# Scatter-add of 65,536 edges on one core: the sort's first pass by quads of chunks, its ranks by a ReLU, and a new order of the dense slots

## The chip, the cores and the metric

One core of a Trainium2 chip runs the kernel. The metric is the device time of one execution in microseconds. Before the change it is 392.3 us, the median of 3 runs (391.73 to 395.86).

## What is computed

```python
num_nodes, num_edges, dim = 4096, 65536, 128
for i in range(len(edge_index_src)):
    output[edge_index_dst[i]] += node_features[edge_index_src[i]]
```

Sources and destinations are random node numbers (64-bit in memory, of which the low word is used); features and output are float32, 4096 x 128.

## The kernel before, in words

Nodes are counted in blocks of 128, so an edge has a source block and a destination block (32 of each) and a place within each. The kernel never adds edge by edge. It sorts the edges by destination block, and then makes each block of output by matmuls.

**The features.** X is cut into three bf16 parts, kept negated in the tile x3 and, for the gathers, in a DRAM copy x3d. `x_part(i, v)` (L172) makes part v of quarter i: ScalarE writes the bf16 part (L174); for v = 0 and 1 a GpSimd DMA adds it into the float32 tile xf, which leaves the residual (L176); after part 2, SyncE writes the quarter to x3d.

**Pass 1** sorts by destination block. The 65,536 edges lie as 128 partitions x 512 columns, padded to 528: 24 chunks of 22 columns, six "quads" q of four chunks. For each chunk a one-hot over the 32 destination blocks is built (`oh1s`, 32 VectorE compares for each of two halves of the chunks, L153). An edge's rank is the number of earlier edges in its chunk with the same block: the running count over the columns is made for half 0 by VectorE adds (L357) and for half 1 by TensorE (`counts`, L213), then VectorE multiplies the counts by the one-hot (L236) and TensorE adds over the blocks (L239), which leaves each edge's own rank (`ranks`). `spread1` (L226) multiplies the one-hot by the edge's code and source block. `move1` (L271) then sends each edge to the partition of its rank: VectorE builds a one-hot of the rank, 128 x 2816 for one of the four chunks of a quad (tile p, helper `onehot`, L258), and 22 matmuls per chunk use it as the weights. ScalarE copies the result to sa (codes) and sbk (source blocks).

**Gathers** serve output blocks 0 to 7. `serve(q)` makes the indices from sa and sbk (`gather_keys`), GpSimd issues four indirect DMAs per group (L299; 48 groups in six buffers, which share their pool with xf), VectorE builds a one-hot of the destinations (ohg) and TensorE adds the rows up (`gather_sum`, L313).

**Pass 2 and the dense slots** serve output blocks 8 to 31, in four groups (`GROUPS`). `pass2(g)` is a generator, and each `on(g)` runs it to its next `yield`. In turn: one-hots over the source blocks (oh2, 32 compares, L411); counts by TensorE (psb, L418); v2 and a running sum of 11 adds (L424, L430); a multiply (L434); ranks by TensorE (psr2, L438); then for each pair of output blocks the one-hots p2b (L258), 48 matmuls (ps2, L462), a ScalarE copy (pa, L467) and two small key tiles (L472, L474). A **slot** makes one output block: VectorE builds the tile oh, two one-hots of 128 x 4096 (`onehots`); `blocks` makes 32 count matrices with TensorE (psa, L489), which ScalarE copies to a (L491); `product` multiplies the a of the slot before by X (pso, L495), alternating with `blocks` eight times; VectorE adds the three parts of the block finished before (res, L321 in `finish`) and SyncE writes it out.

The order is written out by hand: each engine works through its own queue in the order in which the code issues instructions, and an instruction waits only for its inputs and for its buffers. PSUM has eight banks: psi 1, psA 3 (psb1, psc, psr, psa), misc 1, psg 1, pso 2. At the end VectorE and TensorE make a flag from the ranks (L552 to L559); every engine loads it and would branch to a general path if a bucket had overflowed.

## Time and profile before

| | |
|---|---|
| median of 3 runs | 392.3 us (391.73 to 395.86) |
| the profiled execution | 397.01 us, its span 395.4 us |
| busy: PE, DVE, ACT, POOL | 315.8, 303.5, 146.1, 226.8 us |
| mean granted TensorE clock | 0.886 |
| instructions in the span | 7887 |

The span runs from the first to the last instruction that the profile shows; the execution's own time is 1.6 us more. PE is TensorE's matmuls and PEld its weight loads, DVE is VectorE, ACT ScalarE, POOL GpSimd and SP SyncE. In the slices each digit is a fortieth of the span. In the groups of instructions, columns are line, engine, operation, tiles and count, then busy us and mean ns of one, then the idle time before them with what ended it. Instructions of one engine overlap a little, so the distance from one start to the next is less than the mean of one.

### The profile page before, as it was taken

What the parts mean: (1) busy time and instruction counts of PE and PEld (TensorE: products, weight loads), DVE (VectorE), ACT (ScalarE), POOL (GpSimd) and SP (SyncE); (2) the same over time, 40 slices, a digit from 0 to 9 for tenths busy, and PEclk for the clock granted to TensorE, in tenths of its full rate; (3) what the DMA queues carried; (4) which work ended last, traced back from release to release, by engine and by line L of the source; (5) the groups of instructions that cost most, each with busy time, mean ns of one, the idle gap of its engine ahead of it and who ended that gap; (6) DMA issues with size and microseconds to landing.
All of it is one profiled execution on the core that took longest, in us unless ns stands there. A gap on an engine that the chain in (4) does not pass through costs nothing.

```text
span 395.4 us, 7887 instructions
## 1 busy us (share of the span) xinstructions
PE 315.8 (80%) x3274; PEld 229.8 (58%) x3274; DVE 303.5 (77%) x532; ACT 146.1 (37%) x271; POOL 226.8 (57%) x216
## 2 busy tenths in 40 slices
PE   0598765797544679676996999999979999999990
PEld 0255664775442567454674777676747776666650
DVE  4998899899899962838799797678898957676310
ACT  2485400100000044132543445455545455546520
POOL 5832038877812777733588777565785775673000
PEclk9999865676675698896998999999999999999995
DMA  8999732232200233321022333232332332332000
GB/s 245 188 162 158 219 120 70 61 81 70 56 17 12 59 82 81 95 57 48 26 57 76 76 86 87 68 80 69 83 78 68 87 92 68 86 87 66 8 14 10
DMA packets 31014, 32.14 MB, mean 81 GB/s; under 512 B 3904, under 2 KB 27648, under 8 KB 30976
## 3 DMA queue, kind: packets, MB, share of 16 engines
q0 software_dynamic: 17536, 23.08, 27.3%
q1 hardware_dynamic: 13296, 8.01, 7.0%
q8 instruction: 26, 0.43, 0.4%
q10 hardware_dynamic: 144, 0.52, 0.4%
q14 instruction: 12, 0.10, 0.1%
HBM read 22.02 MB, written 5.39 MB: 69 GB/s over the span
## 4 chain that ended last, share of the span: by engine, by line
PE 54%; DVE 39%; issue 3%; DMA 1%; ACT 1%; DVEq 0%
PE pso L495 29%; PE psa L489 10%; DVE p L258 9%; PE psg L313 7%; DVE oh L258 6%; DVE v L226 4%; PE ps L462 4%; DVE cum L430 3%; DVE oh L411 3%; DVE oh L153 3%; PE psr L239 2%; DVE cum L357 2%; PE psr L438 2%; DVE v L424 2%; DVE cum L236 2%
## 5 line engine op out<-in xcount | busy, mean ns | idle before, releaser
L299 POOL DMA_INDIRECT rows<-x3d,gidx x192 | 207.3, 1080 | 119.8 <-issue 71.4
L495 PE MATMUL pso<-x,a 128*128 128x384 bf16 x768 | 160.7, 335 | 0.1
L491 ACT CAST a<-psa 128x512 bf16<-128x512 f32 x192 | 111.7, 588 | 109.5 <-PE psa L489 108.6
L489 PE MATMUL psa<-oh 128*128 128x128 bf16 x768 | 76.1, 223 | 13.9 <-DVE oh L258 13.0
L495 PEld LDWEIGHTS <-a 128*128 128x128 bf16 x768 | 69.3, 100 | 28.0 <-issue 3.0
L489 PEld LDWEIGHTS <-oh 128*128 128x128 bf16 x768 | 59.9, 100 | 40.8 <-DVE oh L258 14.4
L258 DVE TENSOR_TENSOR oh<-psi,slo 128x4096 bf16<-128x4096 uint16 x24 | 54.7, 2278 | 0.0
L258 DVE TENSOR_TENSOR oh<-psi,dlo 128x4096 bf16<-128x4096 uint16 x24 | 54.7, 2277 | 0.0
L313 PE MATMUL psg<-rows,ohg 128*128 128x384 bf16 x192 | 41.2, 359 | 14.4 <-DVE ohg L258 13.1
L321 DVE TENSOR_REDUCE res<-pso 128x128 f32<-128x384 f32 x24 | 13.3, 553 | 40.5 <-PE pso L495 40.5
L271 PE MATMUL psm<-v,p 128*128 128x64 bf16 x512 | 34.1, 239 | 10.4 <-DVE p L258 8.8
L258 DVE TENSOR_TENSOR p<-psi,rank 128x2816 bf16<-128x2816 uint16 x24 | 37.5, 1614 | 3.7 <-ACT rank L243 3.7
L271 PEld LDWEIGHTS <-p 128*128 128x128 bf16 x512 | 30.8, 121 | 14.1 <-DVE p L258 13.3
L313 PEld LDWEIGHTS <-ohg 128*128 128x128 bf16 x192 | 19.2, 106 | 28.7 <-DVE ohg L258 14.0
L258 DVE TENSOR_TENSOR p2b<-psi,rank 128x768 bf16<-128x768 uint16 x48 | 23.3, 547 | 14.2 <-PE ps L462 7.4
L176 POOL DMA_DIRECT2D xf<-x x8 | 14.7, 2278 | 13.6 <-ACT x L174 12.2
L462 PEld LDWEIGHTS <-p2b 128*128 128x128 bf16 x576 | 20.0, 102 | 1.8 <-issue 0.3
L258 DVE TENSOR_TENSOR ohg<-psi,gkey 128x512 bf16<-128x512 uint16 x48 | 18.2, 412 | 0.0
L277 ACT CAST sa<-psm 128x128 bf16<-128x128 f32 x6 | 1.6, 266 | 43.4 <-PE psm L271 43.4
L462 PE MATMUL ps<-v,p2b 128*128 128x32 bf16 x480 | 16.9, 197 | 0.0
L174 ACT ACTIVATE x<-xf 128x1024 bf16<-128x1024 f32 x12 | 12.4, 1055 | 7.5 <-DMA xf<-in_node_features_dram 7.5
L411 DVE TENSOR_SCALAR oh<-sbk 128x96 bf16<-128x96 bf16 (+1 forms) x128 | 14.0, 209 | 1.3 <-ACT sbk L278 1.3
(78 smaller groups left out, 234.6 us busy)
## 6 DMA issues: line engine op xcount, KB each, us to landing
xf<-x POOLq DMA_DIRECT2D x8, 512.0 KB, 8.9
x3d<-x SPq DMA_DIRECT2D x4, 768.0 KB, 8.7
rows<-x3d,gidx POOLq DMA_INDIRECT x192, 2.9
xf<-in_node_features_dram SPq DMA_DIRECT2D x4, 512.0 KB, 7.5
out_dram<-res SPq DMA_DIRECT2D x32, 64.0 KB, 1.8
raw<-in_edge_index_src_dram ACTq DMA_DIRECT2D x1, 512.0 KB
raw<-in_edge_index_dst_dram SPq DMA_DIRECT2D x1, 512.0 KB, 5.1
x3d<-zrow SPq DMA_DIRECT2D x1, 96.0 KB, 5.7
```

The source lines that it names most:

```text
L176: G.dma_start(out=xf[i][:], in_=part, accum_op=OP.add)
L226: V.tensor_tensor(out=v1[q][:, :, k], in0=oh1[q // QH][:, :, q % QH], in1=key[:, q, :, None, :].to_broadcast([P, NJ, NB, 4]), op=OP.mult)
L258: V.tensor_tensor(out=dst.rearrange("p i (m k) -> p i m k", k=2), in0=io.rearrange("p i (m k) -> p i m k", k=2), in1=keys2[:, :, None, :]. ...
L271: PE.matmul(out=psm[:, l * 64:(l + 1) * 64], lhsT=p1[:, l % 2, j, :], rhs=v1[q][:, j, :, :, l].rearrange("p k b -> p (k b)"), start=j == j ...
L299: G.indirect_dma_start(out=t[:, l, :], out_offset=None, in_=x3d[:, :], in_offset=bass.IndirectOffsetOnAxis(ap=gidx[:, place(q).start + l, ...
L313: PE.matmul(out=psg[d][:, :3 * P], lhsT=oh[:, l, :], rhs=t[:, l, :], start=q == 0 and l == 0, stop=q == NQ - 1 and l == 3)
L321: V.tensor_reduce(out=res[:], in_=pso[:, :3 * P].rearrange("p (v f) -> p f v", v=3), op=OP.add, axis=AX.X, negate=True)
L411: V.tensor_single_scalar(out=oh2[:, :, :, s, :], in_=sbk[:, :, ds].rearrange("p c (i k) -> p c i k", k=4), scalar=float(s + 1), op=OP.is_e ...
L462: PE.matmul(out=ps2[:, d % per * NB:(d % per + 1) * NB], lhsT=p2b[d % 2][:, c, :], rhs=v2[:, c, d // 4, :, d % 4], start=c == 0, stop=c == ...
L489: PE.matmul(out=psa[:, i * P:(i + 1) * P], lhsT=oh[0][:, s, :], rhs=oh[1][:, s, :], start=True, stop=True)
L491: S.copy(out=a[:, k * 4:k * 4 + 4, :], in_=psa[:].rearrange("p (s m) -> p s m", s=4))
L495: PE.matmul(out=pso[:, :3 * P], lhsT=a[:, s, :], rhs=x3[:, s, :, :].rearrange("p v f -> p (v f)"), start=s == 0, stop=s == NB - 1)
```

## The change

Pass 1 is done quad by quad. For each quad VectorE builds one one-hot with the helper `onehot` (one instruction of 128 x 2816, which reads the PSUM copy of iota) in place of the compares. TensorE sums each column over the partitions (`pst`, 22 matmuls of one column), VectorE takes a running sum of the 22 totals (`scan`), and TensorE forms the counts in PSUM from the matrix `early`, which is the strict triangle with 4096 on the diagonal, plus the totals of the columns before. ScalarE evicts them with ReLU and a bias of -4096, so that only an edge's own block keeps a count, its rank; the running adds and the multiply of VectorE are gone. The adds over the blocks, the spread, and the move remain, with other layouts: blocks are innermost now, so the move's right-hand side is contiguous.

The residuals of X are made by 16 GpSimd `tensor_tensor` adds of 128 x 512 in place of eight accumulating DMAs. In the slots, VectorE builds the tile oh for slot i+1 before TensorE's slot i, the table `STEPS` says which step of which pass-2 group runs in which slot, GROUPS becomes (4, 4, 8, 8), keys are made pair by pair, and the gather sums come last in a slot while their one-hots are built earlier (`prepare`). The flag is made one slot before the last. PSUM: psA 2, psg 2.

```diff
-GROUPS = (4, 8, 8, 4)
+GROUPS = (4, 4, 8, 8)
+STEPS = {0: [(1, 2)], 1: [(1, 2)], 2: [(1, 0)], 3: [(1, 0), (2, 1)], 4: [(2, 2)], 5: [(2, 1)],
+         6: [(2, 0)], 7: [(2, 0)], 9: [(2, 0), (3, 1)], 11: [(2, 0)], 12: [(3, 2)], 13: [(3, 1)],
+         14: [(3, 0)], 16: [(3, 0)], 18: [(3, 0)], 20: [(3, 0)]}
...
         if v < 2:
-            G.dma_start(out=xf[i][:], in_=part, accum_op=OP.add)
+            for h in range(2):
+                bs = slice(h * BX // 2, (h + 1) * BX // 2)
+                G.tensor_tensor(out=xf[i][:, bs], in0=xf[i][:, bs], in1=part[:, bs], op=OP.add)
...
+    def oh1s(q):
...
+        onehot(oh1q(q), kd[q][:], NL, NB)
+        pst = ps.tile([P, 512], F32, name="pst", tag="pso")
+        for j in range(NJ):
+            PE.matmul(out=pst[:, j:j + 1],
+                      lhsT=oh1q(q)[:, 4 * j:4 * j + 4, :].rearrange("p l b -> p (l b)"),
+                      rhs=ones[:, :1], start=True, stop=True)
...
+    def scan(q):
...
+        V.tensor_tensor_scan(out=sums[q][:], data0=ones[:, :NJ], data1=pst[:, :NJ], initial=0.0,
+                             op0=OP.mult, op1=OP.add)
...
+    def counts(q):
...
+        for j0 in range(0, NJ, 4):
+            n = min(4, NJ - j0)
+            psc = ps.tile([P, 512], F32, name="psc", tag="psA")
+            PE.matmul(out=psc[:, :n * P], lhsT=early[:],
+                      rhs=oh1q(q)[:, 4 * j0:4 * (j0 + n), :].rearrange("p t b -> p (t b)"),
+                      start=True, stop=j0 + n == 1)
+            for j in range(max(j0, 1), j0 + n):
+                PE.matmul(out=psc[:, (j - j0) * P:(j - j0 + 1) * P],
+                          lhsT=sums[q][:, j - 1:j].to_broadcast([P, P]), rhs=identb[:],
+                          start=False, stop=j == j0 + n - 1)
+            S.activation(out=cum[:, :, 4 * j0:4 * (j0 + n)], func=RELU, bias=minus[:],
+                         in_=psc[:, :n * P].rearrange("p (t b) -> p b t", b=NB))
+            yield
...
+        for b in range(NB):
+            PE.matmul(out=psr[:, :NL], lhsT=identb[:], rhs=cum[:, b, :],
+                      start=b == 0, stop=b == NB - 1)
...
+    for q in range(3):
+        dst_keys(q)
+    x_part(0, 0)
+    oh1s(0)
+    codes()
+    x_part(1, 0)
+    oh1s(1)
+    scan(0)
...
+    def during(q):
+        def step(l):
+            if q + 2 < NQ:
+                count(q + 2, 2 if l < 3 else 99)
+            if q == 0:
+                x_part(*((2, 1), (3, 1), (0, 2), (1, 2))[l])
+            elif q == 1 and l < 2:
+                x_part(2 + l, 2)
+        return step
+    for q in range(NQ):
+        move1(q, during(q))
+        if q + 3 < NQ:
+            oh1s(q + 3)
+        if q + 1 < NQ:
+            spread1(q + 1)
...
+        if q + 3 < NQ:
+            scan(q + 3)
+        if q >= 3:
+            add_up(2 * q - 5)
...
+    for slot, (g, i) in enumerate(flat_slots):
+        steps = STEPS.get(slot, ())
+        n = n0 + (len(order) - n0) * (slot + 1) // slots
+        for pg in pending:
+            on(pg)
+        pending = [pg for pg, k in steps if k == 0]
+        prepare(n)
+        cur = oh
+        if slot + 1 < slots:
+            oh = onehots(*flat_slots[slot + 1])
+        for pg, k in steps:
+            for _ in range(max(k - 1, 0)):
+                on(pg)
+                on(pg)
+            on(pg)
+        finish()
...
+        for k in range(8):
+            blocks(k, cur, a)
+            if prev is not None:
+                product(k, prev[1], prev[2])
...
+        for pg, k in steps:
+            on(pg)
+        add_up(n)
+        prev = (first[g] + i, a, pso)
+        if slot == slots - 2:
+            flag()
```

How it moves the queues is shown at three places, each before and then changed. The first is VectorE from the one-hot of the last edges to the first one-hots of the move (p); cum, v, oh and sums are pass 1's tiles, and the numbers behind names are buffers.

```order
L153 TENSOR_SCALAR oh_131<-kd_124 128x66x4 x32
L226 TENSOR_TENSOR v_243<-oh_130,ka 128x22x128
L226 TENSOR_TENSOR v_243<-oh_130,kb 128x22x128
L357 TENSOR_TENSOR cum_210<-cum_210,oh_130 128x384 x4
L226 TENSOR_TENSOR v_250<-oh_130,ka 128x22x128
L357 TENSOR_TENSOR cum_210<-cum_210,oh_130 128x384 x8
L226 TENSOR_TENSOR v_250<-oh_130,kb 128x22x128
L357 TENSOR_TENSOR cum_210<-cum_210,oh_130 128x384 x9
L236 TENSOR_TENSOR cum_210<-cum_210,oh_130 128x4224 x2
L258 TENSOR_TENSOR p_486<-psi,rank_236 128x2816 x2
```

```order
L196 TENSOR_TENSOR oh_292<-psi,kd_129 128x2816
L257 TENSOR_TENSOR v_317<-oh_147,ka 128x88x32
L257 TENSOR_TENSOR v_317<-oh_147,kb 128x88x32
L220 SCALAR_TENSOR_TENSOR sums<-ones,pst 128x22
L196 TENSOR_TENSOR p_408<-psi,rank_284 128x2816
L196 TENSOR_TENSOR p_408<-psi,rank_284 128x2816
L196 TENSOR_TENSOR p_489<-psi,rank_284 128x2816 x2
L196 TENSOR_TENSOR oh_292<-psi,kd_130 128x2816
L257 TENSOR_TENSOR v_614<-oh_147,ka 128x88x32
L257 TENSOR_TENSOR v_614<-oh_147,kb 128x88x32
L220 SCALAR_TENSOR_TENSOR sums<-ones,pst 128x22
L196 TENSOR_TENSOR p_620<-psi,rank_399 128x2816
```

The 21 running adds and the multiplies are gone, the next quads' one-hots stand between the moves, and ahead of each quad's first p stands a scan (L220), which reads TensorE's pst of a later quad.

The second is ScalarE in the same stretch; x is a part of X, cum the evicted counts, rank the copied ranks.

```order
L174 ACTIVATE x_199<-xf 128x8x128 x4
L185 ACTIVATE kb<-raw 128x528
L186 ACTIVATE ka<-raw 128x528
L200 CAST cum_210<-psb_212 128x384
L215 CAST cum_211<-psc 128x384 x4
L174 ACTIVATE x_199<-xf 128x8x128
```

```order
L236 ACTIVATE cum<-psc,minus 128x32x16 x5
L236 ACTIVATE cum<-psc,minus 128x32x8
L245 CAST rank_284<-psr 128x88 x2
L178 ACTIVATE x_135<-xf 128x8x128 x2
L236 ACTIVATE cum<-psc,minus 128x32x16 x2
L178 ACTIVATE x_135<-xf 128x8x128
L236 ACTIVATE cum<-psc,minus 128x32x16 x3
L236 ACTIVATE cum<-psc,minus 128x32x8
L245 CAST rank_399<-psr 128x88 x2
L178 ACTIVATE x_135<-xf 128x8x128
```

The parts of X, all four first parts of which stood ahead of everything, now stand in between the evictions of the counts, and half 0's counts go through ScalarE too.

The third is VectorE around the first dense slot; oh is the slot's pair of one-hots, oh_1278 and oh_1774 (32 compares) the start of pass 2 for the second group.

```order
L411 TENSOR_SCALAR oh_1218<-sbk 128x24x4 x32
L411 TENSOR_SCALAR oh_1278<-sbk 128x48x4 x32
L288 TENSOR_SCALAR gslo<-sa 128x32
L289 TENSOR_SCALAR gkey<-sa 128x64
L291 SCALAR_TENSOR_TENSOR gidx<-sbk,gslo 128x32
L424 TENSOR_TENSOR vc_1217<-oh_1218,sa 128x3072
```

```order
L196 TENSOR_TENSOR oh<-psi,slo_1624 128x4096
L196 TENSOR_TENSOR oh<-psi,dlo_1625 128x4096
L504 TENSOR_SCALAR slo_1624<-pa 128x128
L506 TENSOR_SCALAR dlo_1625<-pa 128x128
L196 TENSOR_TENSOR ohg<-psi,gkey 128x512
L196 TENSOR_TENSOR oh<-psi,slo_1624 128x4096
L196 TENSOR_TENSOR oh<-psi,dlo_1625 128x4096
L442 TENSOR_SCALAR oh_1774<-sbk 128x24x4 x32
L456 TENSOR_TENSOR v_1775<-oh_1774,sa 128x3072
```

The second group's start has moved from right behind the first group's to behind the one-hots of the first two slots, and it has four output blocks in place of eight.

More of the change, by code (lines that the diff above doesn't have):

```diff
@@ L247, in place @@
[L247 to L253 removed]
+    oh1, sums, rank1, v1 = {}, {}, {}, {}
     def onehot(dst, keys2, n, m=P, io=None):
```

365 lines of the change are left out of this document (161 added, 204 removed).

## The prediction

> **What bounds the kernel now.** I read the page's engine totals and slices first, then the chain of waits in order of time, then the groups of pass 1, and last the timeline of single engines.
>
> ```profile
> span 395.4 us, 7887 instructions
> PE 315.8 (80%) x3274; PEld 229.8 (58%) x3274; DVE 303.5 (77%) x532; ACT 146.1 (37%) x271; POOL 226.8 (57%) x216
> PE   0598765797544679676996999999979999999990
> DVE  4998899899899962838799797678898957676310
> PEclk9999865676675698896998999999999999999995
> ```
>
> No engine bounds the whole. VectorE is full in the first 14 slices (to 140 us) while TensorE is half busy and its clock is low; from slice 21 (210 us) on TensorE is full. The chain of waits gives the landmarks:
>
> ```profile
> 0.93 5.08 DMA raw<-in_edge_index_dst_dram
> 41.01 3.21 DVE p L258 x3
> 100.79 7.01 DVE oh L411 x64
> 148.50 1.13 PE pso L495 x4
> 181.86 1.28 PE pso L495 x4
> 256.16 0.65 PE pso L495 x4
> 257.03 0.65 PE pso L495 x4
> 379.88 5.21 PE pso L495 x32
> ```
>
> The edges are there at 6.0, the first p of the move starts at 41.0. Pass 1 ends at 100.8, where pass 2 starts its compares. The first product (slot 1) is at 148.5, that of slot 10 at 256.2, and the last product runs from 379.9 to 385.1. So the span falls into 100.8 for pass 1, 47.7 of preparation, 107.7 for slots 1 to 9, 123.7 for slots 10 to 23, and 15.5 of tail. An eighth of a slot takes 0.87 at full clock (256.16 to 257.03), a slot 7.0. Nine slots in 107.7 is far from that: TensorE waits for VectorE there, and pays again when it restarts at a low clock:
>
> ```profile
> 213.72 0.61 PE L489 MATMUL psa<-oh 128*128 128x128 bf16 x4 [3.13 <-DVE oh L258]
> 180.00:182.50 2.50, 1.25 (x7) 0.86 (x8) 2.50 (x5) 0.55 (x1) 1.89 (x3) 0.50 0.35 81
> ```
>
> The first is a TensorE wait of 3.13 us for a slot's one-hots. The second is the window behind such a wait (columns PE, PEld, DVE, ACT and POOL busy, then the granted clock, 0.50): there the four products took 1.28 instead of 0.65. Two or three eighths at that pace cost about 1.7 us.
>
> **Pass 1.** These rows carry it:
>
> ```profile
> L258 DVE TENSOR_TENSOR p<-psi,rank 128x2816 bf16<-128x2816 uint16 x24 | 37.5, 1614 | 3.7 <-ACT rank L243 3.7
> L226 DVE TENSOR_TENSOR v<-oh,ka 128x2816 bf16<-128x2816 bf16 x6 | 9.7, 1616 | 0.0
> L153 DVE TENSOR_SCALAR oh<-kd 128x264 bf16<-128x264 bf16 x64 | 10.9, 298 | 0.0
> L357 DVE TENSOR_TENSOR cum<-cum,oh 128x384 bf16<-128x384 bf16 x21 | 7.5, 357 | 0.6
> L236 DVE TENSOR_TENSOR cum<-cum,oh 128x4224 bf16<-128x4224 bf16 x4 | 9.2, 2349 | 0.0
> L174 ACT ACTIVATE x<-xf 128x1024 bf16<-128x1024 f32 x12 | 12.4, 1055 | 7.5 <-DMA xf<-in_node_features_dram 7.5
> L243 ACT CAST rank<-psr 128x132 bf16<-128x132 f32 x8 | 2.1, 350 | 13.9 <-PE psr L239 13.9
> 141.18 4.04 ACT L491 CAST a<-psa 128x512 bf16<-128x512 f32 x8
> L142 DVE TENSOR_SCALAR raw<-raw 128x528 int32<-128x528 int32 x1 | 0.4, 436 | 3.1 <-DMA raw<-in_edge_index_dst_dram 3.1
> 98.87 1.43 PE psm L271 x21
> 300.70 1.37 PE psr L438 x32
> ```
>
> Removed from VectorE: 10.9 + 7.5 + 9.2 = 27.6 us. Added: six one-hots of 128 x 2816, each like p, whose 24 take 37.5 or 1.55 each: 9.3. Six key shifts of 176 columns are bounded by nothing and by the 0.44 of 528 columns; I take 0.25, 1.5 together. Six scans of 22 columns cost at least 0.1 and at most one 0.44; I take 0.2, 1.2 together. VectorE is thus 15.6 lighter, and a quad costs it seven instructions of 1.55, 10.9.
>
> But the work on the counts moves to ScalarE: 33 evictions of 512 columns (six per quad, the last half as long, so 5.5). A plain one takes 0.50 (4.04 for eight). The ReLU reads PSUM with a stride, as the rank copies do, which need 350 for 132 columns. I bound it by 0.50 and by that rate, 350 / 132 x 512 = 1.36, and take 0.65: a fixed part is most of the 350, and the plain row is the nearer in size. In order, then:
>
> - VectorE from 6.0: three shifts 0.75, a one-hot 1.55, three code operations about 2, a one-hot 1.55, scan, three shifts, scan, one-hot 1.55, spread 3.1: at 18 it waits. TensorE meanwhile sums 44 columns and forms quad 0's counts (5.5 x 1024 columns; at full clock 0.43 for 1024, by row psb further down, 24 x 256 columns in 2.65; at half clock 4.7 in all), ScalarE follows, the 32 rank matmuls take about 1.4 (row psr, 96 columns) to 2.4, then come the next 22 sums that scan(2) reads. The first p starts at about 21.5. It was 41.0, but with the one-hots of all edges done.
> - VectorE then has p(0), one-hot, spread, 10.9, to 32.4. The next scan reads sums that stand behind quad 0's last move in TensorE's queue, and this behind the counts of quads 1 and 2, which ScalarE evicts in between the parts of X. From 20.5 ScalarE has eight of them (8.4 with the row's 1.055), two quads of evictions (7.2), rank copies (1.2), and about 2 of waits for rank matmuls: it ends at 39.5. So VectorE stands for 7.
> - From 39.5: quad 1 10.9 and two sets of gather keys 1.5; from quad 2 on a p has 2688 columns and a quad's four take 5.9, so quad 2 11.3 with keys, quads 3 and 4 9.7 and 10.1 without a one-hot but with gather one-hots, quad 5 5.9; 2.0 from the last p to the compares, as before (98.8 to 100.8). TensorE's share of a quad is 88 moves at 0.068 (row psm) = 6.0, counts 2.4, ranks 1.4 and sums 1.5, 11.3 in all, beside VectorE's, without adding. The sum is 91.
>
> Pass 1 gives **-9.8**. Bounds: with 0.50 for the ReLU, and TensorE and ScalarE nowhere in the way, the 7 us vanish (84); with 1.36, 16.5 evictions up to the scan add 11.7, and nothing is gained.
>
> **The adds on GpSimd.** Sixteen adds of 128 x 512 are in no row. The nearest:
>
> ```profile
> masks.py:199 POOL TENSOR_SCALAR_AFFINE_SELECT ident<-ident 128x128 f32<-128x128 f32 x1 | 0.3, 285 | 0.0
> L163 DVE TENSOR_SCALAR raw<-raw 128x528 int32<-128x528 int32 x1 | 1.0, 1040 | 0.0
> L299 POOL DMA_INDIRECT rows<-x3d,gidx x192 | 207.3, 1080 | 119.8 <-issue 71.4 <-PE psg L313 42.6 <-PE psa L489 4.3
> ```
>
> 285 for 128 columns of one input gives 1.14 for 512; two inputs make at most 2.28; a quarter of the 1.14 is the other end. I take 1.14. ScalarE reads each residual, so the last part of X may wait: after 22.6, when the last first part is written, twelve adds remain, and ScalarE wants the last result at 43.5. That fits while an add costs up to 1.75, and costs nothing; at 2.28 it is 6.5 late. By the Trainium skill (GPSIMD Engine Reference, 3.1 Elementwise) a float32 add of 2048 columns took 4497 ns, so an estimate is 1.1 us here, and by it too the sum stays.
>
> L163 is the same shift as L142 on as many columns and took 1040 instead of 436, while GpSimd was writing descriptors: the two engines get in each other's way. The Trainium skill (SBUF — State Buffer, Who interferes with whom) says that a VectorE instruction with two SBUF inputs and a GpSimd one that reads SBUF exclude each other for their whole length; that is a rule against these adds. It hits only the spreads: the one-hots read iota from PSUM. By that rule the four spreads of 1.6 between 15 and 32 us delay the adds by 6.5 at most, the last one then ends at 22.6 + 13.7 + 6.5 = 42.8, and the sum is the same.
>
> The gathers start when x3d is written, behind ScalarE's last part of X:
>
> ```profile
> 40.81 3.88 ACT L174 ACTIVATE x<-xf 128x1024 bf16<-128x1024 f32 x4
> ```
>
> This part ends at 44.6 after the change, against 44.7, so they move little; 192 of them in 207.3 busy, 119.8 idle, are not the bound.
>
> **Preparation.** Pass 2's first group has the same VectorE work as before, but the second group's stands behind the one-hots of slots 0 and 1. These rows price it and the slots:
>
> ```profile
> 191.26 3.89 DVE L411 TENSOR_SCALAR oh<-sbk 128x192 bf16<-128x192 bf16 x32
> 203.92 5.01 DVE L430 TENSOR_TENSOR cum<-cum,oh 128x512 bf16<-128x512 bf16 x11
> L434 DVE TENSOR_TENSOR cum<-cum,oh 128x6144 bf16<-128x6144 bf16 x2 | 6.7, 3345 | 0.0
> L258 DVE TENSOR_TENSOR oh<-psi,slo 128x4096 bf16<-128x4096 uint16 x24 | 54.7, 2278 | 0.0
> 128.60 1.50 PE ps L462 x48
> 222.36 2.65 PE psr L438 x32
> 198.87 2.78 PE L418 MATMUL psb<-oh,before 128*128 128x256 bf16 x24
> 281.72 1.31 PE psg L313 x8
> ```
>
> For four blocks: compares 3.1 (7.01 for both sets, less 3.89), v2 and multiply 1.7 each (half of 3.3), running sum 3.5, p2b 1.9 per pair. In order from pass 1's end: 3.1 compares, 0.4, 1.7 v2, 1.4 wait for counts, 3.5, 1.7, 3.4 for psr at half clock and its copy, 3.9 for three gather sums at half clock, 1.5 ps, 1.7 copy, keys and gather one-hots, 1.9 p2b, 4.4 oh for slot 0, 0.6, 4.4 oh for slot 1, 3.1 compares of the second group. Only then does TensorE reach its psb, which its queue has ahead of slot 0: 2.6, then slot 0 at ScalarE's pace 4.5, a gather sum and psa 1.1. The sum is 44.9, **-2.8**. If the compares stood behind slot 0 it would be 5.7 less; if TensorE is at half clock still in slot 1, 1.7 more.
>
> **Slots 1 to 9.** TensorE's own work: nine slots 62.8; 14 gather groups at 0.65, 9.1; five ps at 1.5, 7.6; psr 1.4 and 2.65, two psb of 2.65: 88.9. Its waits for VectorE, which may be one slot ahead but not more (oh has two buffers): for the second group's multiply at the end of slot 1, 1.6; for the third group's compares at the end of slot 3, 2.5; for its multiply at the end of slot 5, 4.2, since v2 3.4, running sum 5.0 and multiply 3.3 come on top of three oh of 4.4. Of the two longer ones I let one drop the clock, 1.7. That is 98.9, **-8.8**. Bounds: no wait at all, 88.9, and all as before, 107.7.
>
> **Slots 10 to 23.** 97.7 + 14.6 for gather groups + 2.65 + five ps 7.6 + a wait of 3.9 for the fourth group's multiply (as in slot 5) = 126.5, **+2.8**: the eight-block group now comes last, and its pairs fall here. Bounds +/-4.
>
> **Tail.**
>
> ```profile
> 385.11 0.56 DVE L321 TENSOR_REDUCE res<-pso 128x128 f32<-128x384 f32 x1 [4.64 <-PE pso L495]
> 386.62 0.14 DVE L559 TENSOR_SCALAR flag_i<-fone 1x1 int32<-1x1 f32 x1
> ```
>
> The flag's chain from 385.7 to 386.8 goes under the last slot: **-1.1**, or 0 if the output's DMA is what the end waits for.
>
> **Sum.** -9.8 - 2.8 - 8.8 + 2.8 - 1.1 = -19.7, a span of 375.7. The profiled execution took 1.6 more than its span and, at 397.0, 4.7 more than the median, so I apply the difference to the median: 392.3 - 19.7 = **372.6 us**.
>
> **Rivals.**
> - *ScalarE is not in the way.* Its waits overlap better than I let them, and VectorE leads without a stop: -7 in pass 1, and half of the 10 of waits and clock in slots 1 to 9: 360.6. For it speaks that ScalarE is busy 37%; against it the queue order, eight parts of X amid the evictions. Chance 0.17.
> - *Counts hold pass 1.* ReLU at 1.36, or TensorE at half clock (counts, ranks, sums and moves doubled are more than VectorE's 10.9): the 9.8 are gone, 382.4. For it speaks PEclk of 5 to 7 tenths in those slices; against it that TensorE would be full then. 0.13.
> - *VectorE gets no slot ahead*, because it waits for ps copies and buffers: slots 1 to 9 stay at 107.7, 381.4. For: it must wait for pa after slots 2 and 6. Against: the next oh is built already. 0.08.
> - *GpSimd's adds hold ScalarE* (slower). Place: ScalarE's last parts of X, with quad 3's evictions behind them. Beyond 1.75 us every add costs twelvefold; at 3.4 the gain is gone; at 4, 372.6 + 27 = 399.6. Against: it is over twice the nearest row. 0.07, of which 0.05 beyond 1%.
> - My forecast, 364 to 380: 0.55.
>
> Within 1% (388.4 to 396.2) is about what a measurement can tell from no change. Faster 0.91, same 0.04, slower 0.05. The range goes from 358 (most of what the first rival may give, 372.6 - 7 - 10 = 355.6) to 386 (the second with three clock drops).
>
> **What would show it.** Right: one-hots of 1.55 in pass 1, the first p near 21, a VectorE stop of several us ahead of quad 1's p, compares near 91, first product near 136, slot 10 near 235, last product near 361. Wrong: a ReLU above 1 us; a GpSimd add above 2; a TensorE wait for oh in slots 1 to 9; the first p after 30.

## The result, and the profile after

| | before | predicted | after |
|---|---|---|---|
| median of all runs, us | 394.08 (4 runs) | 372.6 (358 to 386) | 368.78 (4 runs, 368.19 to 369.46) |
| ratio to before | 1 | | 0.938, 95% interval 0.931 to 0.945 |
| pass 1, to the compares of pass 2 | 100.8 | 91.0 | 87.5 |
| preparation, to slot 1's first product | 47.7 | 44.9 | 42.9 |
| slots 1 to 9 | 107.7 | 98.9 | 98.0 |
| slots 10 to 23 | 123.7 | 126.5 | 129.5 |
| tail, from the start of the last 32 products | 15.5 | 14.4 | 8.6 |
| span of the profiled execution | 395.4 | 375.7 | 366.4 |

The change is 6% faster, within the range. In a later session it took 367.64 us beside 396.3 for the kernel before. In some sessions every kernel, the one before included, took about a fifth longer (before: 481 to 484) from some 55 us of the span on; of the runs there I read what lies before 55 us and single places named below. Where a run is set against the changed kernel of another session (367.6 to 368.8, before 394 to 396), the difference is good to about 2 us.

The page of the changed kernel, totals and three slice rows (slices of 9.2 us):

```profile
span 366.4 us, 8352 instructions
PE 299.4 (82%) x3527; PEld 219.8 (60%) x3527; DVE 287.0 (78%) x476; ACT 160.2 (44%) x297; POOL 224.5 (61%) x225
PE   0768867656373597979989999997799999999996
DVE  4982899999759689699994799659994959687721
PEclk9978988978565699989999999999899999999999
```

VectorE lost 16.5 us of busy time (303.5 before), near the 15.6 worked out for pass 1. TensorE's fell by as much (315.8 before), most of it in the moves, below. TensorE is at 7 to 9 tenths from the slice at 128 us on; before, it was full only from 210 on. The chain of waits, in order of time, gives the landmarks of the table:

```profile
87.45 3.16 DVE oh L442 x32
228.39 0.65 PE pso L530 x4
357.85 5.21 PE pso L530 x32
363.08 0.56 DVE res L333
```

What VectorE does and waits for up to quad 2 (five rows of its timeline; in brackets the idle time before a row and what ended it), and GpSimd beside it:

```profile
13.54 1.91 DVE L257 TENSOR_TENSOR v<-oh,ka 128x2816 bf16<-128x2816 bf16 x1
15.37 2.57 DVE L257 TENSOR_TENSOR v<-oh,kb 128x2816 bf16<-128x2816 bf16 x1
19.41 6.19 DVE L196 TENSOR_TENSOR p<-psi,rank 128x2816 bf16<-128x2816 uint16 x4
37.60 0.20 DVE L220 TENSOR_TENSOR_SCAN sums<-ones,pst 128x22 bf16<-128x22 bf16 x1 [7.40 <-PE pst L211]
49.30 5.92 DVE L196 TENSOR_TENSOR p<-psi,rank 128x2688 bf16<-128x2688 uint16 x4
```

```profile
12.81 3.66 POOL L182 TENSOR_TENSOR xf<-xf,x 128x512 f32<-128x512 f32 x2 [1.24 <-ACT x L178]
```

The first p starts at 19.4 (predicted 21.5, before 41.0). The stop of 7.40 us ahead of quad 1's p is there, where and as long as predicted (7). Behind it VectorE's timeline has no wait over 0.25 us up to the last move: from quad 1 on it is full, with quad 2's p at 49.3. TensorE's waits of over 1.3 us from 120 us to the end (its timeline) are these five:

```profile
122.69 2.74 PE L449 MATMUL psb<-oh,before 128*128 128x128 bf16 x24 [9.39 <-DVE oh L442]
139.25 1.53 PE L474 MATMUL psr<-cum,identb 128*128 128x96 bf16 x32 [2.18 <-DVE cum L470]
162.15 4.46 PE L449 MATMUL psb<-oh,before 128*128 128x256 bf16 x24 [2.45 <-DVE oh L442]
184.65 2.82 PE L474 MATMUL psr<-cum,identb 128*128 128x192 bf16 x32 [1.40 <-DVE cum L470]
259.07 1.44 PE L530 MATMUL pso<-x,a 128*128 128x384 bf16 x4 [4.98 <-DVE res L333]
```

All five come from counting work of a later group, as the prediction had them in slots 0, 1, 3, 5 and 13; none is a slot's own one-hots. In the fifth a product needs a buffer that res frees, and on VectorE res stands behind that group's values v2 and running sum (250.2 to 258.5 us), not behind its multiply. The third and the fifth are paid twice. The view by stretches shows the clock right behind them (the column ahead of the DMA share and GB/s):

```profile
162.15:166.61 4.46, 4.46 (x26) 3.32 (x27) 4.46 (x6) 0.00 (x0) 0.00 (x0) 0.62 0.06 18
259.07:262.00 2.93, 2.93 (x13) 1.59 (x13) 2.93 (x4) 0.59 (x1) 2.32 (x3) 0.52 0.45 113
```

At a mean clock of 0.62 the 24 sums took 4.46 instead of the 2.78 of before, and at 0.52 the first four products 1.44 instead of 0.65. The operations that were new, by groups (instructions | busy, mean ns of one | idle before):

```profile
L236 ACT ACTIVATE cum<-psc,minus 128x512 bf16<-128x512 f32 (+1 forms) x36 | 22.0, 656 | 12.2 <-PE psc L233 11.8
L182 POOL TENSOR_TENSOR xf<-xf,x 128x512 f32<-128x512 f32 x16 | 19.8, 1275 | 11.3 <-ACT x L178 11.3
L280 PE MATMUL psm<-v,p 128*128 128x64 bf16 x512 | 20.6, 200 | 4.9 <-DVE p L196 4.8
```

The ReLU took 0.66 (taken: 0.65), the add 1.28 (1.14). The moves of quads took 20.6 for 512, 0.040 each, not the 0.068 that I had taken from before.

### The profile page after: what moved, and what is told of

Its sections match the earlier page's. It is cut to its first block, busy times and chain, and to the rows that moved or that the text cites. A ratio compares the mean times of both kernels' runs of the same rounds, so it can differ in the third digit from the quotient of the medians.

```text
span 366.4 us, 8352 instructions
## 1 busy us (share of the span) xinstructions
PE 299.4 (82%) x3527; PEld 219.8 (60%) x3527; DVE 287.0 (78%) x476; ACT 160.2 (44%) x297; POOL 224.5 (61%) x225
## 4 chain that ended last, share of the span: by engine, by line
PE 55%; DVE 36%; ACT 5%; DMA 1%; issue 1%; DVEq 0%
PE pso L530 27%; DVE oh L196 10%; PE psa L524 9%; DVE p L196 8%; PE psg L325 6%; PE ps L496 4%; DVE cum L465 3%; DVE v L257 3%; DVE oh L442 3%; PE psr L474 3%; PE psb L449 2%; ACT cum L236 2%; DVE v L456 2%; PE psr L241 1%; ACT x L178 1%; DVE cum L470 1%
## 5 line engine op out<-in xcount | busy, mean ns | idle before, releaser
L306 POOL DMA_INDIRECT rows<-x3d,gidx x192 | 199.8, 1041 | 101.2 <-issue 48.1
L530 PE MATMUL pso<-x,a 128*128 128x384 bf16 x768 | 156.3, 328 | 5.5 <-DVE res L333 5.5
L196 DVE TENSOR_TENSOR p<-psi,rank 128x2688 bf16<-128x2688 uint16 (+1 forms) x24 | 36.1, 1566 | 0.0
L236 ACT ACTIVATE cum<-psc,minus 128x512 bf16<-128x512 f32 (+1 forms) x36 | 22.0, 656 | 12.2 <-PE psc L233 11.8
L182 POOL TENSOR_TENSOR xf<-xf,x 128x512 f32<-128x512 f32 x16 | 19.8, 1275 | 11.3 <-ACT x L178 11.3
L280 PE MATMUL psm<-v,p 128*128 128x64 bf16 x512 | 20.6, 200 | 4.9 <-DVE p L196 4.8
L449 PE MATMUL psb<-oh,before 128*128 128x128 bf16 (+1 forms) x96 | 12.3, 309 | 14.7 <-DVE oh L442 11.8
L280 PEld LDWEIGHTS <-p 128*128 128x128 bf16 x512 | 18.6, 103 | 6.9 <-DVE p L196 6.5
L496 PEld LDWEIGHTS <-p2b 128*128 128x128 bf16 x576 | 19.7, 101 | 3.6 <-DVE p2b L196 2.1
L233 PEld LDWEIGHTS <-sums 128*128 128x128 bf16 x126 | 12.1, 116 | 14.4 <-issue 6.6
L449 PEld LDWEIGHTS <-before 128*128 128x128 bf16 x96 | 10.0, 127 | 17.2 <-DVE oh L442 12.7
```

The costliest lines, as they stand in the source:

```text
L182: G.tensor_tensor(out=xf[i][:, bs], in0=xf[i][:, bs], in1=part[:, bs], op=OP.add)
L196: V.tensor_tensor(out=dst.rearrange("p i (m k) -> p i m k", k=2), in0=io.rearrange("p i (m k) -> p i m k", k=2), in1=keys2[:, :, None, :]. ...
L236: S.activation(out=cum[:, :, 4 * j0:4 * (j0 + n)], func=RELU, bias=minus[:], in_=psc[:, :n * P].rearrange("p (t b) -> p b t", b=NB))
L280: PE.matmul(out=psm[:, l * 64:(l + 1) * 64], lhsT=p1[:, l % 2, j, :], rhs=v1[q][:, 4 * j + l].rearrange("p k b -> p (k b)"), start=j == 0, ...
L306: G.indirect_dma_start(out=t[:, l, :], out_offset=None, in_=x3d[:, :], in_offset=bass.IndirectOffsetOnAxis(ap=gidx[:, place(q).start + l, ...
L449: PE.matmul(out=psb[:, h * W:(h + 1) * W], lhsT=before[:], rhs=flat2(oh2)[:, h * NH + c], start=c == 0, stop=c == NH - 1)
```

## Experiments

Two theories were open. Theory A: the prediction's terms, each at its size, the tail for 1.1. Theory B: the tail is the miss, since what the program does with the flag after it is written was most of the empty end. Beside them each term of pass 1 and the lead of a slot has its own rival.

**1. The flag early in the kernel before** (`e1_before_flag_early`). The chain becomes a function and is called in the loop:

```
             prev = (first[g] + i, a, pso)
+            if slot == slots - 1:
+                flag()
         on(g + 1, 99)
```

> The kernel before with one edit: the flag's chain stands after the gather blocks of slot 23, ahead of the last 32 products, as it does after the change; nothing else is altered. Theory A, the prediction's term: only the chain of small instructions from 385.7 to 386.8 goes under the products, so the time falls by about 1.1 us. Theory B: what the program does with the flag after it is written (the engines load it to branch on it) is most of the 8.6 us that the profile shows empty from 386.8 to 395.4, and runs beside the last products once the flag is early, so the time falls by 6 to 7 us and the span ends about 3 us after the last reduction of res.

Measured: 393.0 us, ratio 0.997 (0.993 to 1.002): no difference. The call stood one slot earlier than meant, behind slot 22's blocks (slot was counted up above it). VectorE and TensorE there, and the end of the chain of waits:

```profile
372.04 0.28 DVE L510 TENSOR_REDUCE fone<-psf 1x1 f32<-1x128 f32 x1 [7.56 <-PE psf L508]
376.95 0.61 PE L489 MATMUL psa<-oh 128*128 128x128 bf16 x4 [4.94 <-DVE oh L258]
```

```profile
387.33 5.21 PE pso L495 x32
392.57 0.56 DVE res L321
```

VectorE waits 7.56 us for the transposed maximum, which stands behind slot 22's blocks in TensorE's queue. Slot 23's one-hots stand behind that wait, so TensorE then waits 4.94 for them. The last 32 products start at 387.3 instead of 379.9, 7.4 later, but the end is 395.9: the tail is 8.6 instead of 15.5. The 7 us were gained at the end and lost in slot 23. That the total stands still is no evidence for theory A.

**2. The same, past the one-hots** (`e9_before_flag_early2`), in one of the slower sessions:

```
             oh = onehots(g, i)
             finish()
+            if slot == slots - 1:
+                flag()
```

> The kernel before with the flag's chain moved again, now right behind the one-hots of slot 23 on VectorE and ahead of slot 23's blocks on TensorE, so that no one-hots stand behind its wait for the transposed maximum (in the first try the chain stood after slot 22's blocks, VectorE waited 7.6 us for that transpose and slot 23's one-hots came 5 us late). Theory B (loading the flag after it is written is what the 8.6 us of empty end were): slot 23 starts as it did before plus about 1 us, the end follows the last reduction by about 3 us, and the time falls by 5 to 7 us against the kernel before. Theory A (chain alone): by about 1 us.

Measured: ratio 0.979 (0.959 to 1.000), 469.1 against 480.9; the interval reaches 1, so the total alone decides nothing, and the tail does. Slot 23 is no longer held up (VectorE waits 0.58 for the transpose, TensorE for no one-hots), and the page's first line and the end of the chain read:

```profile
span 466.0 us, 7887 instructions
```

```profile
457.37 5.21 PE pso L495 x32
462.61 0.56 DVE res L321
```

The tail is 8.6 here too, and the span ends 2.8 us after the last reduction. In place and size this is theory B: with the flag written early, all but 2.8 us of the empty end is gone.

**3. The flag late in the changed kernel** (`e2_after_flag_late`):

```
-        if slot == slots - 2:
-            flag()
     finish()
     for k in range(8):
         product(k, prev[1], prev[2])
     done.append((prev[0], prev[2]))
     finish()
+    flag()
```

> The changed kernel with the flag's chain put back behind the last slot's reduction and output. Theory A (chain alone): plus 1.1 us, about 370. Theory B (the load of the flag costs the end): plus 6 to 7 us, about 375, with 8 to 9 us of empty span behind the flag's last instruction.

Measured: 379.22 us, 10.4 over the changed kernel (368.78, another session). The page's first line and two rows of the chain:

```profile
span 378.4 us, 8353 instructions
```

```profile
364.13 0.56 DVE res L333
366.68 0.14 DVE flag_i L545
```

The spans differ by 12.0: 1.0 lies ahead of the last products, 2.1 is the chain (364.7 to 366.8), and 8.8 is an empty stretch of 11.6 us behind the flag in place of the 2.8 behind the last reduction. So theory B has the sign and the place, and its 6 to 7 are too little here: in the changed kernel the early flag is worth about 10 us.

What stands in the empty stretch is in the kept traces, among the instructions that the views leave out (start in us of the span, then duration):

| | before | flag late (run 3) | changed |
|---|---|---|---|
| flag written, end | 386.76 | 366.82 | 350.05 |
| GpSimd loads the flag | 386.79, 0.50 | 366.86, 0.50 | 350.09, 0.50 |
| GpSimd `INC_SWDGE_SEM` | 388.27, 1.38 | 368.31, 1.91 | 351.55, 1.91 |
| GpSimd `DRAIN` | 389.68, 4.89 | 370.25, 7.10 | 353.49, 7.10 |
| span ends | 395.4 | 378.4 | 366.4 |

Each of the five engines loads the flag in about half a microsecond and branches. GpSimd, behind its branch, then ends its part of the program with these two instructions, 6.3 us in the kernel before and 9.0 in the changed one, and the engines meet behind them, 0.8 to 1.0 us ahead of the end. So it is not the loads that fill the stretch: GpSimd's end waits for the flag, and with the flag early it runs beside the last products. In all fourteen kept traces the two instructions take 1.38 and 4.89 us where X's residuals are made by DMAs (before, and runs 1, 2, 8 and 9) and 1.91 and 7.10 where GpSimd adds them. Those 2.7 us, brought by the adds, are nearly all of the 2.9 by which the stretch of run 3 is longer than that of the kernel before. Why the adds lengthen GpSimd's end, nothing here shows.

**4. No slot ahead** (`e3_after_own_slot`):

```
-    oh = onehots(0, 0)
...
-        cur = oh
-        if slot + 1 < slots:
-            oh = onehots(*flat_slots[slot + 1])
+        cur = onehots(g, i)
```

> The changed kernel with VectorE's lead of one slot taken away: a slot's one-hots are built in the slot itself, behind whatever VectorE did in the slot before. Theory (the lead is what slots 1 to 9 gained): TensorE waits for oh at several of the early slots, 2 to 4 us each with low-clock products behind, and slots 1 to 9 go from 98.0 back to about 107; preparation loses nothing, since slot 1's one-hots no longer stand ahead of the second group's compares (4.4 earlier); slots 10 to 23 change by less than 3. In all plus 5 to 9 us, about 376. Rival: the lead does nothing, TensorE's waits for the groups' multiplies are the whole cost of these slots: 366 to 370, with slots 1 to 9 at 98.

Measured: 429.28 us, 60 over the changed kernel and 8.5% over the one before (ratio 1.086, 1.077 to 1.095). Preparation takes 38.3 us, 4.6 less, as expected; slots 1 to 9 take 123.5 instead of 98.0, slots 10 to 23 170.1 instead of 129.5. Rows of the view of waits from slot 1 on (us in total, times, longest), without and then with the slot ahead:

```profile
DVE slo L504 <- ACT pa L500: 78.1, 10, 9.5
PE psa L524 <- DVE oh L196: 56.8, 13, 6.0
```

```profile
DVE slo L504 <- ACT pa L500: 29.8, 8, 4.9
```

In this order of steps pass 2's products ps, which place the edges of a pair of output blocks, stand behind a slot's blocks on TensorE, so VectorE waits for their copy pa until the slot ends. With the next one-hots already built this wait is free. Without them the 4.4 us of one-hots come behind the wait, and TensorE stands 13 times for 56.8 us. Theory and rival both had this far too small: the kernel before builds a slot's one-hots in the slot itself too, and by the same view its TensorE waited for them 5 times, 13.0 us in all, and VectorE twice for pa, 7.8. Its steps stand elsewhere. The new order needs the lead; without it, it is worse than the old one.

**5. X's parts later** (`e4_after_x_late`), and with them the first two sets of gathers:

```
-    count(1, 2)
-    x_part(0, 1)
     count(1)
-    x_part(1, 1)
     scan(2)
...
         def step(l):
             if q + 2 < NQ:
                 count(q + 2, 2 if l < 3 else 99)
-            if q == 0:
-                x_part(*((2, 1), (3, 1), (0, 2), (1, 2))[l])
-            elif q == 1 and l < 2:
-                x_part(2 + l, 2)
+            if q in (1, 2):
+                x_part(l, q)
...
-        if q == 1:
+        if q == 2:
             serve(0)
-        if 1 <= q < NQ - 1:
+            serve(1)
+        if 2 <= q < NQ - 1:
             serve(q)
```

> The changed kernel with the parts of X moved in ScalarE's order: the second parts during quad 1's move, the third during quad 2's, so that six of them no longer stand ahead of quad 1's ranks; the gathers of the first two gather groups are issued two quads later. Theory of the prediction (ScalarE's queue, evictions amid parts of X, makes VectorE stand 7.4 us ahead of quad 1's p): six parts at 1.06 leave this queue, the stop falls to 1 to 3 us and quad 1's p starts near 33 instead of 37.6; some of that may be lost later, as the first gather comes at about 60 instead of 49. Rival 1 (TensorE at low clock sets quad 1's counts and sums): the stop stays at 6 to 7 us. Rival 2 (VectorE bounds the rest anyway and the late gathers hold nothing): the end moves by all that the stop loses, to 362 to 364 us. If the later evictions of X collide with quads 3 and 4, the gain is given back and the time is 368.

Measured: 373.6 us, 4.8 over the changed kernel.

```profile
33.77 0.20 DVE L220 TENSOR_TENSOR_SCAN sums<-ones,pst 128x22 bf16<-128x22 bf16 x1 [3.92 <-PE pst L211]
63.02 1.11 POOL L306 DMA_INDIRECT rows<-x3d,gidx  x1 [14.40 <-issue]
110.47 0.23 DVE L500 TENSOR_SCALAR slo<-pa 128x128 uint16<-128x128 uint16 x1 [4.81 <-ACT pa L496]
```

The stop goes from 7.40 to 3.92 us, less of a fall than expected (1 to 3 left), and quad 1's p starts 3.8 earlier, at 33.9: six of the eight parts of X make about half of the stop. The first gather is issued at 63.0 instead of 49.2, and GpSimd, at one gather in 1.25 us, does not catch up by the preparation: the chain of waits runs over its gathers from 85 to 105 us, VectorE waits 4.81 for pa (2.95 in the changed kernel), and preparation takes 47.4 instead of 42.9. The early parts of X cost 3.8 at quad 1 and buy more than that. The edit moves the gathers with the parts, so the two are not told apart.

**6. One spread more per quad** (`e5_extra_spread`; the same values written twice), in a slower session:

```
-        for k, key in ((0, kab), (1, kb[:])):
+        for k, key in ((0, kab), (1, kb[:]), (1, kb[:])):
```

> The changed kernel with the second product of each of pass 1's six spreads done a second time into the same place (same result): about 1.55 us more VectorE per quad, nothing else. Prediction's theory (VectorE stands idle ahead of quads 0 and 1, and from quad 2 on it is what sets each p): the extra ones ahead of the stops vanish, the four for quads 2 to 5 add 1.55 each, the compares start 6 us later (93.5), and this reaches the end: about 375. Rival 1 (ScalarE or TensorE sets the later quads too): compares at 87.5 to 89. Rival 2 (VectorE sets everything from the start): plus 9.3, compares at 96.8.

```profile
37.53 0.20 DVE L220 TENSOR_TENSOR_SCAN sums<-ones,pst 128x22 bf16<-128x22 bf16 x1 [4.67 <-PE pst L211]
50.90 5.92 DVE L196 TENSOR_TENSOR p<-psi,rank 128x2688 bf16<-128x2688 uint16 x4
```

The extra spread ahead of quad 0 uses up the wait of 1.35 there (p at 19.57 instead of 19.41), and the one ahead of quad 1 vanishes in its stop (4.67 left of 7.40, p at 37.65). Quad 2's p comes at 50.90 instead of 49.30, later by the one spread behind quad 1's p. So VectorE sets quad 2 and does not set quads 0 and 1, as predicted. For quads 3 to 5, the compares and the end (479.75) this run can't be read; that VectorE sets them rests on its full timeline, above.

**7. Each ReLU eviction twice** (`e6_relu_twice`; same values), in a slower session:

```
-            S.activation(out=cum[:, :, 4 * j0:4 * (j0 + n)], func=RELU, bias=minus[:],
-                         in_=psc[:, :n * P].rearrange("p (t b) -> p b t", b=NB))
+            for _ in range(2):
+                S.activation(out=cum[:, :, 4 * j0:4 * (j0 + n)], func=RELU, bias=minus[:],
+                             in_=psc[:, :n * P].rearrange("p (t b) -> p b t", b=NB))
```

> The changed kernel with each ReLU eviction of pass 1 done twice into the same place (same result): 33 more ScalarE instructions of 0.66, 22 us in all, four or so us per quad. Prediction's theory (ScalarE's queue up to the second scan of sums, with eight parts of X and two to three quads of evictions, sets quad 1's p; later VectorE does): 3 quads of evictions ahead of quad 1's p, so the stop of 7.4 us grows by 8 to 11 to 15 to 18, p of quad 1 at about 47, compares near 97, end near 378. Rival (VectorE alone sets pass 1, or TensorE's clock does): p of quad 1 moves by under 4 and the end by under 4.

```profile
23.42 0.20 DVE L220 TENSOR_TENSOR_SCAN sums<-ones,pst 128x22 bf16<-128x22 bf16 x1 [5.32 <-PE pst L211]
50.92 0.20 DVE L220 TENSOR_TENSOR_SCAN sums<-ones,pst 128x22 bf16<-128x22 bf16 x1 [16.59 <-PE pst L211]
```

The first p comes 4.1 us later (23.5), quad 1's 13.3 later (51.0), with a stop of 16.59. The stop grew by 9.2, within the expected 8 to 11; quad 1's p is 4 later than expected (47), since the first p moved too, which the expectation had left out. Both are far from the rival's 4: up to quad 1's p the chain runs through ScalarE's evictions, 13.3 us for the 16.5 extra ones or some 0.8 each. The end (497.25) is again not read.

**8 and 9. X's residuals by DMA** (`e7_dma_residuals` and `e12_dma_residuals_again`, the same kernel, both in slower sessions):

```
-            for h in range(2):
-                bs = slice(h * BX // 2, (h + 1) * BX // 2)
-                G.tensor_tensor(out=xf[i][:, bs], in0=xf[i][:, bs], in1=part[:, bs], op=OP.add)
+            G.dma_start(out=xf[i][:], in_=part, accum_op=OP.add)
```

> The changed kernel with the residuals of X formed as before, by accumulating DMAs issued on GpSimd, instead of by the sixteen GpSimd adds; all else as changed. Theory (the adds lie beside other work and cost nothing, as the prediction has it, and the DMAs did too): no difference beyond 1 us, 368 to 370. Rival 1 (the adds hold VectorE's spreads, 1.91 and 2.57 instead of 1.6): VectorE's spread of quad 0 is back at 1.6 each but the first p does not depend on it alone, so the gain is under 2 us: 367 to 369. Rival 2 (a DMA takes 9 us to land where two adds take 2.6, and ScalarE reads each residual in a fixed place of its queue): ScalarE stands behind the DMAs, the stop ahead of quad 1's p grows by 3 to 8 us and the end goes to 372 to 377; the adds are then a real part of the gain.

> The changed kernel with the residuals of X by accumulating DMAs again. In the first run of it quad 1's p stood where it stands with the adds (38.0 against 37.7), the spreads of quad 0 took 1.61 and 1.62 instead of 1.91 and 2.57, and ScalarE then waited 0.5, 1.2 and 4.0 us for residuals, after which quad 2's p came at 54.1 instead of 49.4; from 55 us on that chip was slow. Theory: these 4.7 us reach the end, 371 to 374. Rival (VectorE or TensorE has slack later in pass 1, so that the delay is absorbed): 367 to 369.

The first run of the two, VectorE and then ScalarE:

```profile
13.75 1.61 DVE L255 TENSOR_TENSOR v<-oh,ka 128x2816 bf16<-128x2816 bf16 x1
15.29 1.62 DVE L255 TENSOR_TENSOR v<-oh,kb 128x2816 bf16<-128x2816 bf16 x1
53.63 0.18 DVE L293 TENSOR_SCALAR gslo<-sa 128x32 uint16<-128x32 uint16 x1 [4.42 <-ACT sa L282]
54.13 5.92 DVE L194 TENSOR_TENSOR p<-psi,rank 128x2688 bf16<-128x2688 uint16 x4
```

```profile
41.35 1.06 ACT L178 ACTIVATE x<-xf 128x1024 bf16<-128x1024 f32 x1 [1.16 <-DMA xf<-x]
47.57 1.06 ACT L178 ACTIVATE x<-xf 128x1024 bf16<-128x1024 f32 x1 [4.01 <-DMA xf<-x]
```

Quad 0's spreads are back at 1.61 and 1.62, and the first p does not move (19.7). ScalarE stands behind the last residuals, VectorE waits 4.42 for the copy sa that follows them in ScalarE's queue, and quad 2's p starts at 54.1, in the second run at 54.6, instead of 49.3: 4.8 to 5.3 us later. So the adds are worth about 5 us at quad 2; rival 2 had the mechanism and put it one quad too early. What is left of this at the end stays open: the same kernel took 479.97 and 459.16 us in sessions where the kernel before took 483.45 and 484.06.

**10, 11 and 12. Pass 2's counting work spread out** (10 is `e8_steps_spread`, in a slower session; 11 is the same as `e11_steps_spread_again`, beside 12, `e10_after_again`, which is the changed kernel itself). The counting steps of the third and fourth group are spread over two slots each, slot 0's blocks go ahead of the second group's sums, and a later group's values are formed with its first pair:

```
-STEPS = {0: [(1, 2)], 1: [(1, 2)], 2: [(1, 0)], 3: [(1, 0), (2, 1)], 4: [(2, 2)], 5: [(2, 1)],
-         6: [(2, 0)], 7: [(2, 0)], 9: [(2, 0), (3, 1)], 11: [(2, 0)], 12: [(3, 2)], 13: [(3, 1)],
+STEPS = {0: [(1, 1)], 1: [(1, 2)], 2: [(1, 0)], 3: [(1, 0), (2, 1)], 4: [(2, 1)], 5: [(2, 1)],
+         6: [(2, 0)], 7: [(2, 0)], 9: [(2, 0), (3, 1)], 10: [(3, 1)], 11: [(2, 0)], 12: [(3, 1)],
...
-        for i in range(gk):
-            V.tensor_tensor(out=v2[:, :, i], in0=oh2[:, :, i], op=OP.mult,
+        def values():
+            for i in range(gk):
+                V.tensor_tensor(out=v2[:, :, i], in0=oh2[:, :, i], op=OP.mult,
...
+        if g == 0:
+            values()
...
+            if g > 0 and i == 0:
+                values()
```

> A version that may be better: the changed kernel with three changes of order in pass 2. Slot 0's blocks and slot 1's stand ahead of the second group's sums in TensorE's queue; the third and fourth groups' counting work is spread over two slots each instead of standing in one; the values of a later group are formed with its first pair instead of ahead of its counts, 1.7 to 3.4 us less VectorE work before the counts' multiply. Theory (TensorE's waits of 9.4, 2.2, 2.5, 1.4 and 5.0 us for VectorE at these groups, with products at low clock behind some, are a matter of what VectorE has ahead, not of its sum of work): most of the 20 us of waits go, first product 3 to 8 us earlier, the wait of 5 us in slot 13 gone: 357 to 362. Rival (VectorE's whole work up to slot 13 is the bound, so that the waits only move to other slots): 366 to 370.

> The changed kernel as it is, beside the next one and the kernel before on one chip. In the last two calls every kernel, the one before among them, took about a fifth longer from some 55 us of the span on. If this chip is like the first, 368 to 370; if it is like those of the last two calls, the change keeps its ratio of 0.94 only as far as the extra time is in proportion, 450 to 475.

> The version with pass 2's counting work spread over more slots, beside the changed kernel on one chip. Theory (TensorE's waits for VectorE are a matter of what VectorE has ahead): 8 to 12 us under the changed kernel in the same call. Rival (VectorE's sum of work up to slot 13 is the bound): within 2 us of it.

Measured: 352.10 us (351.59 to 352.48) against 367.64 in the same session, 15.5 less, ratio to before 0.888 (0.882 to 0.895). In the slower session the ratio to before was 0.956 (0.944 to 0.968). The page, and all of TensorE's waits of over 1.3 us from 120 us on:

```profile
span 350.9 us, 8357 instructions
PE 299.0 (85%) x3527; PEld 220.9 (63%) x3527; DVE 286.8 (82%) x476; ACT 160.2 (46%) x297; POOL 229.3 (65%) x225
```

```profile
120.89 2.72 PE L449 MATMUL psb<-oh,before 128*128 128x128 bf16 x24 [3.68 <-DVE oh L442]
154.98 4.12 PE L449 MATMUL psb<-oh,before 128*128 128x256 bf16 x24 [2.46 <-DVE oh L442]
```

Both engines are busy for as long as in the changed kernel (299.0 and 286.8 against 299.4 and 287.0). Three of the five waits are gone and the first fell from 9.39 to 3.68. Against the changed kernel's trace in the same session, preparation is 4.9 us shorter, slots 1 to 9 4.6, slots 10 to 23 6.1; pass 1 is 1.5 longer and the tail equal. The rival (VectorE's sum of work is the bound) has fallen. The theory's 8 to 12 were too little: behind pass 1 the gain is 15.6, of which 14.4 are the waits that went, and the rest fits the low-clock products behind the wait of slot 13, which are gone too. The three changes of order were made at once, so none of them is priced alone.

## Why the prediction was right, and what was mis-sized

- **Pass 1: -9.8 predicted, -13.3 measured.** The structure was right: ScalarE up to quad 1 (run 7), then VectorE (run 6), a stop of 7.4 for 7. The first p came 2.1 earlier: VectorE's first scan was done 1.0 earlier than my rows add up to, and quad 0's ranks ran without the low clock that I had let in (32 products in 1.41 instead of 2.4), while its counts did take the half-clock time (4.8 us for my 4.7). The two sets of gather keys cost 0.8 instead of 1.5 beside quad 1, and the last 0.6 are the moves: the last 21 took 0.80 in place of 1.43 (last section).
- **Adds on GpSimd: 0 predicted, no wait of ScalarE for them seen.** What the DMAs would have cost here, about 5 us at quad 2 (runs 8 and 9), the prediction did not ask. Both engines do slow each other: VectorE's spreads took 1.91 and 2.57 beside adds and 1.61 and 1.62 without them (run 8), and the second of the two adds there took 2.54 where the first took 1.16. A scan's wait of 1.35 behind the spreads hid it. By the Trainium skill (SBUF — State Buffer, Who interferes with whom) the two should exclude each other for their whole length; the trace agrees: the first add ends at 13.97, the first spread at 15.45, the second add at 16.46 and the second spread at 17.94, so each ends 1.48, 1.01 and 1.48 behind the one before it, a little less than it takes alone.
- **Preparation: -2.8 predicted, -4.8 measured.** The order worked out holds, and the terms were on the slow side: 1.5 up to the second group's compares (ranks with their copy 2.7 for 3.4, gather sums 3.6 for 3.9) and most of the rest in slot 0 with its gather sum (4.9 for 5.6). The price of slot 1's one-hots ahead of those compares, 4.4, is 4.6 by run 4.
- **Slots 1 to 9: -8.8 predicted, -9.7 measured.** Waits of 1.6, 2.5 and 4.2 were 2.2, 2.5 and 2.0 (0.56 and 1.40), with one drop of the clock (1.7). What the lead is worth was mis-sized in the rival: I priced its lack at 9 us, and it is 60 in this order.
- **Slots 10 to 23: +2.8 predicted, +5.8 measured.** The wait of slot 13 was 4.98 for 3.9, and its low-clock products, about 1.4, were left out. TensorE's own sum, 122.6, was right: run 11, without that wait, took 123.3.
- **Tail: -1.1 predicted, -7.0 measured: the step that failed.** "The flag's chain from 385.7 to 386.8 goes under the last slot: **-1.1**, or 0 if the output's DMA is what the end waits for." I counted the instructions that the views show and gave the 8.6 empty microseconds behind them no cause. They are GpSimd's end of the program, 6.3 us behind its branch on the flag, and the meeting of the engines after it (table of run 3). Runs 1 and 2 take all but 2.8 of them out of the kernel before; run 3 puts a longer stretch into the changed one. The other value that I allowed, 0, had the output's DMA as what the end waits for: in the kernel before its last packet is through at 386.9, 8.5 us ahead of the end.

In all the spans differ by 29.0 for a predicted 19.7. Of the 9.3 between, 5.9 lie in the tail, 3.5 in pass 1, 2.0 in preparation, 0.9 in slots 1 to 9, and slots 10 to 23 take 3.0 of it back; that the sum came this close is in part the luck of the one term with the other sign. The medians differ by 25.3, less than the spans, since the profiled execution of before was one of its longer ones. So the likeliest case came true, with the mechanism of each stage but the last; in the tail the sign was right and its reason was not. The rival without ScalarE in the way did not: its 7 us of stop are there.

## What to carry to other kernels

An empty stretch at the end of a span is a cost like any other: ask what the program still does there that the rows leave out (here GpSimd's end, held by a flag), and let it start earlier, but put the flag where nothing stands behind its wait. Count a wait together with what stands behind it on the same engine: building a slot's operands ahead was worth 60 us in this order because long waits stand in front of them. And before lightening an engine that seems full, list the other engine's waits by what is ahead of each: moving the same work cut 15.5 us from an already improved kernel.

## What the runs showed of the hardware

- The moves' products of 64 columns by 128 rows took 34.1 us for 512 before and 20.6 after. Stretches with 21 of them, twice in the kernel before (columns here: length, PE busy, ACT busy, granted clock, DMA share, GB/s; moves alone) and once in the changed one (all engines):

```profile
98.87:100.30 1.43, 1.41 (x21) 0.00 (x0) 1.00 0.29 82
56.80:59.80 3.00, 1.40 (x21) 0.00 (x0) 0.50 0.14 39
```

```profile
86.16:86.96 0.80, 0.80 (x23) 0.73 (x24) 0.60 (x2) 0.00 (x0) 0.49 (x2) 1.00 0.04 12
```

  Before, 21 took 1.4 us at clock 1.00 and at 0.50 alike, so the clock did not set them; after, 0.80 at 1.00, and 21 at a low clock (0.50, from 50.9 us) took 1.30. What the edit changed for them is the moving operand v, which lay with a stride of four elements (the last index l of `v1[q][:, j, :, :, l]`) and is now in one piece (`v1[q][:, 4 * j + l]`). I had carried the old pace over. That the stride is the cause is argued from these rows; no run changed it alone.
- A wait of 2.45 us was followed by a low clock (0.62, above); in run 11 the same products took 4.12 behind 2.46, in run 12 4.46 behind 2.62.
- GpSimd's end of the program took 6.3 us in five traces and 9.0 in nine (1.38 and 4.89, 1.91 and 7.10, table of run 3), the same to the nanosecond within each group; the two groups differ in whether GpSimd adds X's residuals.
- A gather in an unbroken row on GpSimd costs 1.25 us (0.95 busy and 0.30 between), and a start 13.8 us later was not caught up in 40 us.
